# A two-block fp32 network on one core: products of zeros placed in TensorE's foreseen waits, and new tables for the order of the work

## The chip, the cores and the metric

One core of a Trainium2 chip runs the whole network as one program. The metric is device time in microseconds (us) of one execution; less is better. The kernel before has a median of 2796.93 us over three runs, the lowest 2793.36, the highest 2799.09.

## The reference

Batch 1, 512 tokens, width 1024, all in fp32. A first block: a mixer (dilated causal attention beside HGRN2, 8 heads each) and a mixture of experts. Then a second block with two layers over the same 512 tokens and 256 tokens of context: an even layer (MLA attention beside gated linear attention, GLA) and an odd layer (gated delta net, GDN), each with an MLP of width 4096.

```python
def first_block(x, ...):
    h = rmsnorm(x, norm1_g[layer])
    proj = h @ w_in[layer]
    ...
    mixed = jnp.concatenate([y_attn, y_hgrn], axis=-1)
    x = x + mixed @ w_out[layer]
    h2 = rmsnorm(x, norm2_g[layer])
    x = x + hier_moe(h2, ...)
    return rmsnorm(x, norm_f_g)

def second_block(x, c, ctx, ...):
    for layer in range(2):
        ml = jnp.split(silu(c) @ ada_w[layer] + ada_b[layer], 6)
        mc = jnp.split(silu(c_ctx) @ ada_w[layer] + ada_b[layer], 6)
        a_lat = modulate(rms_norm(h_lat, norm1_w[layer]), ml[0], ml[1])
        a_ctx = modulate(rms_norm(h_ctx, norm1_w[layer]), mc[0], mc[1])
        o_lat, o_ctx = even_mixer(...) if layer == 0 else odd_mixer(...)
        h_lat = h_lat + ml[2] * o_lat
        h_lat = h_lat + ml[5] * sq_relu_mlp(modulate(rms_norm(h_lat, norm2_w[layer]), ml[3], ml[4]), ...)
        ...
    return rms_norm(h_lat, final_norm)
```

`hier_moe` picks one group of 8 experts out of 4 for each token and in it the best two experts, and runs SwiGLU experts of width 512 on the tokens that chose them, in blocks of 128.

## The kernel before

Activations lie transposed in SBUF: features on the 128 partitions, tokens along the free dimension. Large products are made from three fp32r products each: activation and weight are split into a high part in fp32r and the rest (`xh`, `xl` and `wh`, `wl`), and xh·wh, xl·wh and xh·wl are summed in PSUM. A weight comes as a tile `raw` of 128x512 fp32 (256 KB) from memory; ScalarE (ACT) makes `wh` by a cast and VectorE (DVE) `wl` by a subtraction. The experts' weights (`mw`) and those of the modulation (`aw`) are used as they are, in fp32. All transfers but the gathers go out on SyncE's queue (SP); the gathers of token rows (`xg`) are indirect transfers that GpSimd (POOL) issues. A norm's sum of squares is a product of the squares `sq` with a matrix of ones (`const_all`), a pair of products to a norm of 128x512.

No engine's order is written by hand. Class `Rec` stands in for the engines: each operation is recorded as a `Unit` with its engine, its cost, its operands' tiles and a rank of the part it belongs to (table `RK`). `Rec.schedule` is a list scheduler: it runs a model of the five engines, takes at each step the unit that can start first on an engine (by rank, by order, by the weights in `ORDER`), honours limits on how many tiles of a name a part may hold (table `CAPS`), and returns one order of all units. It foresees when each unit starts, with a model of TensorE's clock among it. `Rec.flush` then emits the units in this order, so that each engine runs its instructions in it; every recorded operation is issued from one line, L336 in `emit` (L346 in the changed kernel). What an engine finds not ready it waits for, with everything behind it.

There are two flushes. The first part holds the mixer (`mix1`), the experts (`moe`, with the parts `ada0`, `evenC` and six of eight parts of the context's first MLP, `mlpC`, recorded among them as other work) and ends in a loop over overflow blocks (L1347) that runs zero times here. The second part holds `comb` (the sum of the experts' outputs), `evenL`, `ada1`, `mlpD` (the other two parts of mlpC), `oddC`, `mlp0`, `oddL` (GDN over the 512 tokens), `mlp1` and `end` (the final norm).

PSUM has 8 banks, all of one tag; each tile `pq` is a target of products. In the order's rows below, names carry the number of their tile.

Of the kernel before, what the change touches and what calls it, by code (L numbers as in the profile page):

```python
# [7 lines left out]
F32 = mybir.dt.float32  # L8
F32R = mybir.dt.float32r
# [7 lines left out]
P = 128  # L17
# [225 lines left out]
class Eng:
# [7 lines left out]
class Rec:  # L251
# [30 lines left out]
    def call(self, eng, method, a, k):  # L282
# [11 lines left out]
        out = writes[0] if writes else reads[0]  # L294
# [32 lines left out]
        u.uses += [(r, False) for r in reads] + [(w, True) for w in writes]
# [142 lines left out]
    def schedule(self):  # L470
# [33 lines left out]
        mode = None  # L504
# [28 lines left out]
        while len(order) < N:  # L533
# [112 lines left out]
    def flush(self):  # L646
# [233 lines left out]
class B:  # L880
# [9 lines left out]
    def start(self):  # L890
# [1371 lines left out]
def prep2(inp):  # L2262
# [20 lines left out]
    for z in range(2):  # L2283
# [29 lines left out]

RK = {"ada0": (7.4, 12.23), "ada1": (2.99, 8.19), "comb": (0.87, -1.0), "end": 3.3, "evenC": (1.97, 5.86),
      "evenC.gla": (-0.22, 6.0), "evenC.mla": (0.78, 7.24), "evenC.out": (6.2, 7.24), "evenL": (1.45, -0.02),
      "evenL.gla": (2.99, 2.44), "evenL.mla": (6.32, 0.83), "evenL.out": (4.6, 5.81), "mix1": (1.08, -0.1),
      "mix1.attn": (1.38, 5.7), "mix1.hgrn": (1.28, 7.3), "mix1.out": (6.5, 4.8), "mix1.qkv": (1.28, 2.69), "mlp0":
      (2.43, 5.08), "mlp1": (1.09, 6.3), "mlpC": (0.68, -0.4), "mlpD": (-0.31, -1.2), "moe": (1.04, 12.78), "oddC":  # L2320
      (6.88, 2.34), "oddC.inv": (0.63, 8.01), "oddC.inv0": (2.85, 6.33), "oddC.inv1": (5, 6.3), "oddC.opd": (4.6,
      8.42), "oddC.step": (4.6, 4.43), "oddC.v": (7.67, 8.09), "oddL": (1.79, 0.87), "oddL.g": (3.37, 2.62),
      "oddL.inv": (2.71, 3.97), "oddL.inv0": (1.66, -1.69), "oddL.inv1": (-1.23, -1.0), "oddL.opd": (12.48, 6.4),
      "oddL.out": (1.79, 0.8), "oddL.q": (5.6, 2.12), "oddL.step": (1.97, -0.27), "oddL.v": (-1.1, 0.9), "zero":
      (-0.31, 9.99)}
CAPS = {".xc": 68, ":x2561": 15, "ada0.ar": 153, "ada0.pq": 3, "ada0:pq": 13, "ada1.aw": 18, "ada1.pq": 11, "ada1:t":
      11, "comb.pq": 21, "comb.rs": 34, "comb.ru": 99, "comb.sq": 12, "comb.yy": 17, "comb:pq": 3, "comb:t": 204,
      "end.pq": 34, "end.rs": 11, "end.ru": 9, "end.sq": 4, "end.y": 36, "end:pq": 508, "end:t": 4, "evenC.ao": 66,
      "evenC.cqk": 68, "evenC.gA": 10, "evenC.gS": 8, "evenC.gb": 1, "evenC.gg": 24, "evenC.gkN": 10, "evenC.gke": 11,
      "evenC.gki": 1, "evenC.go": 5, "evenC.gqk": 6, "evenC.gt": 14, "evenC.gv": 4, "evenC.kT": 7, "evenC.kpe": 11,  # L2330
      "evenC.kx": 45, "evenC.ms": 24, "evenC.pT": 24, "evenC.pb": 90, "evenC.pq": 189, "evenC.qT": 2, "evenC.raw": 3,
      "evenC.rs": 33, "evenC.ru": 1, "evenC.s": 4, "evenC.sg": 25, "evenC.sq": 22, "evenC.vN": 9, "evenC.wh": 2,
      "evenC.wl": 51, "evenC.xh": 22, "evenC.xl": 72, "evenC:pq": 4, "evenC:s": 3, "evenC:t": 26, "evenL.gA": 17,
      "evenL.gS": 7, "evenL.gb": 15, "evenL.gg": 10, "evenL.gkN": 10, "evenL.gke": 1, "evenL.go": 17, "evenL.gst": 47,
      "evenL.gt": 49, "evenL.gv": 8, "evenL.kT": 541, "evenL.kc": 176, "evenL.kpe": 13, "evenL.kx": 26, "evenL.ms": 2,
      "evenL.pT": 8, "evenL.pa": 125, "evenL.pb": 12, "evenL.pq": 20, "evenL.qT": 4, "evenL.qps": 6, "evenL.raw": 3,
      "evenL.s": 11, "evenL.sg": 25, "evenL.sq": 56, "evenL.vc": 13, "evenL.wh": 2, "evenL.wl": 72, "evenL.y": 8,
# [7 lines left out]
      2, "mlp1:pq": 67, "mlpC.hl": 19, "mlpC.pq": 7, "mlpC.raw": 4, "mlpC.rl": 12, "mlpC.rs": 12, "mlpC.ru": 5,  # L2345
      "mlpC.sq": 11, "mlpC.wh": 6, "mlpC.xh": 42, "mlpC.xl": 28, "mlpC.y": 36, "mlpC:pq": 37, "mlpC:t": 58, "mlpD.hh":
      5, "mlpD.hl": 6, "mlpD.pq": 34, "mlpD.raw": 2, "mlpD.rl": 1265, "mlpD.wh": 41, "mlpD.wl": 63, "mlpD.xh": 23,
      "mlpD.xl": 4, "mlpD:pq": 1, "moe.BV": 12, "moe.EV": 128, "moe.RO": 3, "moe.RV": 48, "moe.hidT": 3, "moe.hr": 17,
      "moe.lT": 1, "moe.pq": 21, "moe.rs": 13, "moe.rt": 17, "moe.ru": 12, "moe.sg": 69, "moe.sq": 9, "moe.xg": 44,
      "moe.ys": 18, "moe:m4x": 11, "moe:m4y": 8, "moe:pq": 25, "oddC.A": 23, "oddC.Ax": 17, "oddC.G": 79, "oddC.TTx":  # L2350
      369, "oddC.Tx": 8, "oddC.Z": 7, "oddC.chb": 17, "oddC.hA": 3, "oddC.hB": 16, "oddC.hT": 137, "oddC.hp": 12,
      "oddC.kN": 9, "oddC.kP": 22, "oddC.kT": 3, "oddC.kbg": 1, "oddC.ke": 24, "oddC.kx": 12, "oddC.lab": 15,
      "oddC.pq": 28, "oddC.raw": 5, "oddC.rq": 52, "oddC.rs": 108, "oddC.ru": 5, "oddC.s": 32, "oddC.sg": 145,
      "oddC.u": 66, "oddC.vP": 12, "oddC.vT": 18, "oddC.vb": 19, "oddC.vs": 17, "oddC.wh": 25, "oddC.wl": 6,
      "oddC.wx": 58, "oddC.xl": 41, "oddC.y": 19, "oddC:pq": 7, "oddC:s": 14, "oddC:t": 45, "oddC:z4": 13, "oddL.A":
      7, "oddL.Ax": 38, "oddL.D": 7, "oddL.G": 15, "oddL.S": 76, "oddL.Tx": 18, "oddL.Z": 29, "oddL.eg": 56,
      "oddL.gT": 5, "oddL.gm": 40, "oddL.gn": 71, "oddL.hA": 10, "oddL.hT": 11, "oddL.hs": 22, "oddL.kN": 22,
      "oddL.kP": 120, "oddL.kT": 16, "oddL.kbg": 48, "oddL.ke": 17, "oddL.kx": 125, "oddL.o": 48, "oddL.pq": 74,
      "oddL.qP": 11, "oddL.qT": 78, "oddL.qkx": 9, "oddL.qx": 5, "oddL.raw": 7, "oddL.ri": 3, "oddL.rq": 1, "oddL.rs":
      65, "oddL.ru": 6, "oddL.s": 94, "oddL.sg": 13, "oddL.sq": 11, "oddL.u": 14, "oddL.vP": 15, "oddL.vT": 11,  # L2360
      "oddL.vb": 36, "oddL.vs": 14, "oddL.wh": 40, "oddL.wl": 57, "oddL.wx": 5, "oddL.xh": 70, "oddL.xl": 67,
      "oddL:pq": 8, "oddL:s": 6, "oddL:z4": 19, "zero.zero": 6, "zero:t": 34}
# [95 lines left out]
```

## Time and profile before

| | |
|---|---|
| median of 3 runs | 2796.93 us (2793.36 to 2799.09) |
| profiled execution | 2799.62 us |
| span of its instructions | 2797.8 us |
| mean granted clock of TensorE | 0.958 |
| busy: PE, DVE, ACT, POOL | 93%, 55%, 39%, 19% |
| moved by DMA | 503.39 MB, mean 180 GB/s |

The profiled execution is one run with its own time; the span runs from its first instruction to its last. PE is TensorE, PEld its loading of the stationary operand. A clock of 1.00 is 2.4 GHz, 0.50 is 1.2 GHz; a value between them for a stretch is a mean of the two. In a timeline, the end of a product is modelled; how fast products follow each other is read from their starts.

### The profile page before, as it was taken

The numbers are of one execution on the slowest core, as the hardware profiler recorded it, in microseconds if no ns is written. First come the engines' busy times: TensorE is split into PE (matmuls) and PEld (weight loads), VectorE is DVE, ScalarE is ACT, GpSimd is POOL, SyncE is SP. The second block draws the span as 40 slices with busy tenths as digits, with TensorE's granted clock in tenths as the row PEclk, the third lists the DMA queues.
The fourth block names the chain that finished last, engine by engine and source line by source line (L and its number), as shares of the span: only waits on it lengthen the run. The fifth ranks groups of instructions, "written<-read, shape, count | busy, mean of one in ns | idle before, by whom it ended". The sixth has DMA issues, their size and how long they took to land. (4 is left out here: it accounts for less than half of the span.)

```text
span 2797.8 us, 42711 instructions
## 1 busy us (share of the span) xinstructions
PE 2600.4 (93%) x15498; PEld 1906.0 (68%) x15498; DVE 1534.4 (55%) x2837; ACT 1096.3 (39%) x2243; POOL 518.2 (19%) x620
## 2 busy tenths in 40 slices
PE   7999989899999997999899998999898797899997
PEld 5875645445566664678657877888776686688886
DVE  7466432245343334846686875445668858454434
ACT  5346212235332323534455543333464525343321
POOL 1320013010010001112001321100143775010100
PEclk9999989999999999999799999999999788999999
DMA  5137799999999999931102545233324732233221
GB/s 196 54 110 241 271 308 321 298 307 326 379 340 365 378 367 328 380 126 55 47 22 75 171 118 163 85 106 102 93 96 106 193 95 73 79 106 106 87 83 42
DMA packets 323752, 503.39 MB, mean 180 GB/s; under 512 B 79826, under 2 KB 94162, under 8 KB 323026
## 3 DMA queue, kind: packets, MB, share of 16 engines
q1 hardware_dynamic: 318930, 492.23, 53.0%
q0 software_dynamic: 4608, 8.40, 0.8%
q8 instruction: 123, 2.02, 0.3%
q14 instruction: 91, 0.75, 0.1%
HBM read 473.22 MB, written 35.66 MB: 182 GB/s over the span
## 5 line engine op out<-in xcount | busy, mean ns | idle before, releaser
L336 PE MATMUL pq<-xh,wh 128*128 128x512 f32 (+1 forms) x1712 | 630.1, 368 | 33.2 <-ACT xh L336 14.3
L336 PE MATMUL pq<-xh,wl 128*128 128x512 f32 (+1 forms) x1712 | 615.8, 360 | 17.7 <-DVE wl L336 17.6
L336 ACT CAST wh<-raw 128x512 fp32r<-128x512 f32 x676 | 400.0, 615 | 560.4 <-DMA raw<-mlp_w 294.8
L336 PE MATMUL pq<-xl,wh 128*128 128x512 f32 (+1 forms) x1712 | 615.3, 359 | 3.6 <-DVE xl L336 3.6
L336 DVE TENSOR_TENSOR wl<-raw,wh 128x512 fp32r<-128x512 f32 (+1 forms) x676 | 478.4, 732 | 241.3 <-ACT wh L336 159.6
L336 PEld LDWEIGHTS pq<-xh,wh 128*128 128x128 f32 x1712 | 329.0, 192 | 120.3 <-ACT xh L336 33.6
L336 PEld LDWEIGHTS pq<-xh,wl 128*128 128x128 f32 x1712 | 328.5, 192 | 70.9 <-DVE wl L336 23.9
L336 PEld LDWEIGHTS pq<-xl,wh 128*128 128x128 f32 x1712 | 328.6, 192 | 52.4 <-DVE xl L336 5.7
L336 PE MATMUL pq<-hh,wh 128*128 128x512 f32 (+1 forms) x768 | 274.1, 357 | 0.0
L336 PE MATMUL pq<-hl,wh 128*128 128x512 f32 (+1 forms) x768 | 271.4, 353 | 0.0
L336 PE MATMUL pq<-hh,wl 128*128 128x512 f32 (+1 forms) x768 | 271.4, 353 | 0.0
L336 PE MATMUL pq<-mw,xT 128*64 128x512 f32 x1024 | 257.2, 611 | 0.7 <-DMA mw<-w_up 0.7
L336 DVE SCALAR_TENSOR_TENSOR x<-pq,mod,x 128x512 f32<-128x512 f32 x144 | 108.0, 750 | 225.4 <-PE pq L336 225.3
L336 POOL TENSOR_TENSOR rl<-rl 128x512 f32<-128x512 f32 (+1 forms) x96 | 100.2, 1049 | 702.5 <-ACT rl L336 621.2
L336 PEld LDWEIGHTS pq<-hh,wh 128*128 128x128 f32 x768 | 144.8, 189 | 35.9 <-issue 9.2
L336 PEld LDWEIGHTS pq<-hl,wh 128*128 128x128 f32 x768 | 144.9, 189 | 20.1 <-issue 0.2
L336 PEld LDWEIGHTS pq<-hh,wl 128*128 128x128 f32 x768 | 144.9, 189 | 20.0
L336 PEld LDWEIGHTS pq<-mw,xT 128*64 128x64 f32 x1024 | 70.8, 139 | 126.1 <-issue 91.5
L336 PE MATMUL pq<-mw,hidT 128*64 128x512 f32 x512 | 135.9, 604 | 3.2 <-DMA mw<-w_down 2.7
L336 DVE TENSOR_TENSOR hl<-rl,hh 128x512 fp32r<-128x512 f32 (+1 forms) x96 | 68.4, 721 | 97.8 <-ACT hh L336 81.6
L336 ACT ACTIVATE rl<-pq 128x512 f32<-128x512 f32 (+1 forms) x96 | 49.1, 525 | 164.6 <-PE pq L336 164.5
L336 ACT ACTIVATE sq<-x 128x512 f32<-128x512 f32 x64 | 39.2, 629 | 165.2 <-DVE x L336 127.7
(387 smaller groups left out, 3690.0 us busy)
## 6 DMA issues: line engine op xcount, KB each, us to landing
raw<-mlp_w SPq DMA_DIRECT2D x384, 256.0 KB
mw<-w_gate SPq DMA_DIRECT2D x256, 256.0 KB
mw<-w_up SPq DMA_DIRECT2D x256, 256.0 KB
mw<-w_down SPq DMA_DIRECT2D x256, 256.0 KB
aw<-ada_w SPq DMA_DIRECT2D x192, 256.0 KB
raw<-even_w_in SPq DMA_DIRECT2D x72, 256.0 KB
raw<-gdn_w_in SPq DMA_DIRECT2D x72, 256.0 KB
raw<-w_in SPq DMA_DIRECT2D x56, 256.0 KB
```

Source lines behind the costliest of these rows:

```text
L336: return getattr(getattr(self.real, eng), method)(*[f(v) for v in a], **kw)
```

## The change

It does three things. `Rec.call` gives each unit of PE that starts a tile of at least 256 columns (on 128 or 64 partitions) a price for a product of zeros of its shape. `Rec.schedule`, where it foresees that PE will stand idle for over 500 ns ahead of such a unit, puts a number of such products there: as many as fill 0.65 of the foreseen wait, at twice the price if the modelled clock is low, and books them as activity in its model of the clock. `Rec.flush` emits them ahead of the unit, with the unit's own output tile as their target; the unit's first product starts that tile anew, so they leave nothing behind. The zeros are two constant tiles. And the tables `RK`, `CAPS` and one weight of each pair in `ORDER` are new.

```diff
+FILL, SHARE = 500.0, 0.65
...
+            u.fill = (0, 0.0, 0.0)
+            if eng == "tensor" and len(out.shape) == 2 and k.get("start", True) and out.shape[0] in (64, 128):
+
+                n, full = int(out.shape[1]), out.shape[0] == 128
+                if full and n >= 256:
+                    u.fill = n, 13.3 + n / 2.4, n / 2.4
+                elif n >= 256:
+                    u.fill = n, max(224.0, 5.0 + n * 1.667), n / (0.6 if full else 1.2)
+            u.fills = 0
...
             if e == "tensor":
+                if u.fill[0] and st - eng[e] > FILL:
+
+                    slow = 1.0 if all(x[3] for x in clock) else 2.0
+                    u.fills = int(SHARE * (st - eng[e]) / (u.fill[1] * slow))
+                    for i_ in range(u.fills):
+                        at = eng[e] + i_ * u.fill[1] * slow
+                        for g, x in enumerate(clock):
+                            while x[0] < int(at / WINDOW + 0.25 * g):
+                                x[:] = x[0] + 1, x[2], 0.0, x[1] > WARM * WINDOW
+                            x[1] += u.fill[2]
...
             for i in order:
-                for c in self.units[i].calls:
+                u = self.units[i]
+                for _ in range(u.fills):
+                    o = u.calls[0][2][0]
+                    w, x = self.zeros[o.shape[0] == 128 and o.shape[1] >= 256]
+                    self.emit("tensor", "matmul", (o, w[:, :o.shape[0]], x[:, :o.shape[1]]),
+                              dict(start=True, stop=True, skip_group_check=True))
+                for c in u.calls:
                     self.emit(*c)
...
+        z, zr = (self.cp.tile([P, 512], t, name=f"zero{i}") for i, t in enumerate((F32, F32R)))
+        nc.gpsimd.memset(z, 0.0)
+        nc.vector.tensor_copy(zr, z)
+        nc.zeros = [(z, z), (zr, zr)]
...
-RK = {"ada0": (7.4, 12.23), "ada1": (2.99, 8.19), "comb": (0.87, -1.0), "end": 3.3, "evenC": (1.97, 5.86),
+RK = {"ada0": (5.47, 2.26), "ada1": (5.51, 3.96), "comb": (5.41, -0.59), "end": (5.65, 4.62), "evenC": (1.9, 2.93),
...
-CAPS = {".xc": 68, ":x2561": 15, "ada0.ar": 153, "ada0.pq": 3, "ada0:pq": 13, "ada1.aw": 18, "ada1.pq": 11, "ada1:t":
+CAPS = {".xc": 47, ":x2560": 5, "ada0.ar": 1, "ada0.aw": 246, "ada0.pq": 29, "ada0:pq": 75, "ada0:t": 32, "ada1.ar":
...
-ORDER = (9900, 3.991), (3500, 0.097)
+ORDER = (9900, 2.382), (3500, 0.093)
```

Over the whole program PE gets 151 products of zeros at 17 places (106 of 128x512, 41 of 128x256, 4 of 64x512), DVE one copy and POOL one memset; nothing else is added or taken away. 41 of the zeros stand in the first part, 110 in the second. Three places show what moved.

The first gather, on PE, where the routing of the tokens (`rt`, `ar`, `EV`, `BV`) ends and the first gathered rows `xg` are transposed by a product with the unit matrix. Before:

```order
L336 MATMUL pq_3615<-rt_3598,const_all 128x32 x7
L336 MATMUL pq_3661<-const_all,ar_3413 128x128 x4
L336 MATMUL pq_3674<-const_all,ar_3436 128x128 x4
L336 MATMUL pq_3686<-EV_3610,RO_3679 64x16 x32
L336 MATMUL pq_3781<-BV_3763,RV_3758 64x32 x8
L336 MATMUL pq_3831<-const_all,xg_3567 128x128 x4
L336 MATMUL pq_3838<-const_all,xg_3567 128x128 x4
```

Nothing stands between the routing and the first `xg`. In the changed kernel:

```order
L346 MATMUL pq_3673<-rt_3657,const_all 128x32 x7
L346 MATMUL pq_3614<-xh_3455,wh_3563 128x256
L346 MATMUL pq_3614<-xl_3559,wh_3563 128x256
L346 MATMUL pq_3614<-xh_3455,wl_3699 128x256
...
L346 MATMUL pq_3742<-EV_3691,RO_3731 64x16 x32
L346 MATMUL pq_3837<-BV_3817,RV_3812 64x32 x8
L346 MATMUL pq_3614<-xh_3466,wh_3736 128x256
L346 MATMUL pq_3614<-xl_3567,wh_3736 128x256
L346 MATMUL pq_3614<-xh_3466,wl_3848 128x256
...
L346 MATMUL pq_3933<-const_all,xg_3628 128x128 x4
L346 MATMUL pq_3942<-const_all,xg_3628 128x128 x4
```

Products of evenC (`xh`, `xl` with `wh`, `wl`, 128x256) now stand between the routing and the first transposes: 6 ahead of `EV`, and 42 between `BV` and the first `xg` (three of the 42 are shown).

The mixer's output, on PE, from the sum of squares (`sq`) of its norm to the first product of the output matrix (`xh,wh`). Before:

```order
L336 MATMUL pq_2435<-aw_2473,adasc 32x512
L336 MATMUL pq_2435<-aw_2481,adasc 32x512
L336 MATMUL pq_2891<-sq_2562,const_all 128x512
L336 MATMUL pq_2299<-aw_2496,adasc 32x512
L336 MATMUL pq_2299<-aw_2515,adasc 32x512
...
L336 MATMUL pq_2435<-aw_2825,adasc 32x512
L336 MATMUL pq_2435<-aw_2837,adasc 32x512
L336 MATMUL pq_2986<-xh_2948,wh_2872 128x512
```

Twelve small products of the modulation (`aw`) stand between the two. In the changed kernel, from the same sum of squares on:

```order
L346 MATMUL pq_2682<-hA_631,iN_857 64x128
L346 MATMUL pq_2718<-sq_2167,const_all 128x512
L346 MATMUL pq_2682<-hT_659,S_2626 64x32 x2
L346 MATMUL pq_2682<-hT_659,S_2680 64x32 x6
L346 MATMUL pq_2682<-hA_553,iN_810 64x128
L346 MATMUL pq_2682<-hA_631,iN_810 64x128
L346 MATMUL pq_2736<-vm_1487,t_2686 64x256 x2
L346 MATMUL pq_2736<-vm_1541,t_2686 64x256 x2
L346 MATMUL pq_2747<-hT_692,t_2123 128x128 x4
```

In their place stand HGRN2's products (`hT`, `hA`, `vm`), and they go on behind the last row shown here.

The end of GDN, on PE: its last products (`qkx,u`), the sums of squares of its output's norm and the first products of its output matrix (`oh,wh`). Before:

```order
L336 MATMUL pq_22773<-qkx_22750,u_22689 128x128
L336 MATMUL pq_22826<-sq_22820,const_all 128x512
L336 MATMUL pq_22833<-sq_22824,const_all 128x512
L336 MATMUL pq_22927<-oh_22429,wh_22853 128x512
L336 MATMUL pq_22927<-oh_22444,wh_22853 128x512
```

The sums of squares follow the last GDN products, and the output matrix follows them. In the changed kernel, first the same place, then, behind the output matrix, the norm ahead of mlp1 and its first product:

```order
L346 MATMUL pq_22870<-qkx_22810,u_22783 128x128
L346 MATMUL pq_22927<-zero_87 128x512 x16
L346 MATMUL pq_22927<-sq_22922,const_all 128x512
L346 MATMUL pq_22948<-sq_22925,const_all 128x512
L346 MATMUL pq_23048<-zero_87 128x512 x11
L346 MATMUL pq_23048<-oh_22549,wh_22968 128x512
...
L346 MATMUL pq_23333<-zero_87 128x512 x6
L346 MATMUL pq_23333<-sq_23154,const_all 128x512
L346 MATMUL pq_23333<-sq_23330,const_all 128x512
L346 MATMUL pq_23381<-zero_87 128x512 x17
L346 MATMUL pq_23381<-xh_23365,wh_23361 128x512
```

Only the products of zeros are new here: 16 and 11 around the first sums of squares, 6 and 17 around the second.

## Rows read from the trace of the kernel before

**Rows 1.** The page: busy time, and PE's granted clock in 40 slices.

```profile
PE 2600.4 (93%) x15498; PEld 1906.0 (68%) x15498; DVE 1534.4 (55%) x2837; ACT 1096.3 (39%) x2243; POOL 518.2 (19%) x620
...
PEclk9999989999999999999799999999999788999999
```

**Rows 2.** The waits of PE over the span: total us, times, longest.

```profile
PE pq L336 <- DMA xg<-h2d,idx: 18.8, 4, 8.4
PE pq L336 <- DVE sq L336: 18.8, 4, 12.8
...
PE pq L336 <- DMA mw<-w_down: 2.7, 4, 1.5
```

**Rows 3.** Stretches: from:to, us, PE, PEld, DVE, ACT, POOL, clock, DMA share, GB/s.

```profile
350.00:630.00 280.00, 253.13 (x1434) 139.69 (x1434) 93.00 (x230) 71.24 (x151) 47.71 (x63) 0.91 0.91 309
700.00:1050.00 350.00, 346.34 (x2124) 219.28 (x2122) 134.14 (x244) 108.81 (x215) 25.79 (x33) 1.00 1.01 366
2356.00:2371.50 15.50, 4.84 (x8) 1.54 (x6) 12.54 (x29) 10.27 (x38) 6.86 (x15) 0.60 0.13 41
2434.00:2779.00 345.00, 345.00 (x1523) 285.64 (x1522) 159.25 (x229) 114.43 (x197) 42.06 (x34) 1.00 0.27 86
```

**Rows 4.** Timeline of PE, 2416 to 2430: start, us, instruction, [idle before, releaser].

```profile
2419.48 2.91 PE L336 MATMUL pq<-sq,const_all 128*128 128x512 f32 x4 [2.24 <-DVE sq L336]
2427.54 0.80 PE L336 MATMUL pq<-xh,wh 128*128 128x512 f32 x1 [5.16 <-ACT xh L336]
...
2429.31 0.63 PE L336 MATMUL pq<-xh,wl 128*128 128x512 f32 x1
2429.73 0.63 PE L336 MATMUL pq<-xh,wh 128*128 128x512 f32 x1
```

**Rows 5.** Timeline of PE behind the loop, 1079 to 1097.

```profile
1091.97 0.58 PE L336 MATMUL pq<-xh,wh 128*128 128x256 f32 x1 [12.63 <-DMA xv<-mlpx]
...
1094.31 0.41 PE L336 MATMUL pq<-xh,wh 128*128 128x256 f32 x1
1094.52 0.41 PE L336 MATMUL pq<-xl,wh 128*128 128x256 f32 x1
...
1096.39 0.28 PE L336 MATMUL pq<-xh,wl 128*128 128x256 f32 x1
1096.51 0.28 PE L336 MATMUL pq<-xh,wh 128*128 128x256 f32 x1
```

**Rows 6.** Timeline of PE at the start, 0 to 30.

```profile
12.84 3.78 PE L336 MATMUL pq<-sq,const_all 128*128 128x512 f32 x4 [12.84 <-DVE sq L336]
23.16 0.80 PE L336 MATMUL pq<-xh,wh 128*128 128x512 f32 x1 [6.54 <-ACT xh L336]
25.10 0.80 PE L336 MATMUL pq<-xl,wh 128*128 128x512 f32 x1 [1.15 <-DVE xl L336]
```

**Rows 7.** Timeline of PE, sums of squares in the GDN part, at 2155.

```profile
2155.34 1.88 PE L336 MATMUL pq<-sq,const_all 128*128 128x512 f32 x4
```

**Rows 8.** Timeline of PE at the mixer's output, 276 to 283.

```profile
280.95 0.49 PE L336 MATMUL pq<-xh,wh 128*128 128x512 f32 x1 [2.65 <-ACT xh L336]
282.88 0.49 PE L336 MATMUL pq<-xl,wh 128*128 128x512 f32 x1 [1.44 <-DVE xl L336]
```

**Rows 9.** Timeline of PE at the first gather.

```profile
378.85 0.87 PE L336 MATMUL pq<-const_all,xg 128*128 128x128 f32 x3 [8.41 <-DMA xg<-h2d,idx]
```

**Rows 10.** The page: products of the experts' up and gate weights.

```profile
L336 PE MATMUL pq<-mw,xT 128*64 128x512 f32 x1024 | 257.2, 611 | 0.7 <-DMA mw<-w_up 0.7
```

**Rows 11.** Timeline of PE at 1361.

```profile
1370.44 0.80 PE L336 MATMUL pq<-xh,wl 128*128 128x512 f32 x1 [9.02 <-DVE wl L336]
```

**Rows 12.** Timeline of PE at the end of GDN, 2356 to 2371.

```profile
2360.66 3.78 PE L336 MATMUL pq<-sq,const_all 128*128 128x512 f32 x4 [4.39 <-ACT sq L336]
2370.64 1.69 PE L336 MATMUL pq<-oh,wh 128*128 128x512 f32 x2 [6.20 <-ACT oh L336]
```

**Rows 13.** Timeline of PE at the final norm.

```profile
2781.70 3.31 PE L336 MATMUL pq<-sq,const_all 128*128 128x512 f32 x4 [2.24 <-DVE sq L336]
```

More of the change, by code (lines that the diff above doesn't have):

```diff
@@ L233 @@
 class Unit:
-    __slots__ = ("eng", "calls", "cost", "lat", "pred", "succ", "uses", "prio", "npred", "ready", "start", "key", "idx", "refs", "ph", "rank", "late", "part", "need", "extra", "rows", "end", "mode")
+    __slots__ = ("eng", "calls", "cost", "lat", "pred", "succ", "uses", "prio", "npred", "ready", "start", "key", "idx", "refs", "ph", "rank", "late", "part", "need", "extra", "rows", "end", "mode", "fill", "fills")
 LAT = 200.0
@@ L2311, in prep2 @@
     return r
-RK = {"ada0": (7.4, 12.23), "ada1": (2.99, 8.19), "comb": (0.87, -1.0), "end": 3.3, "evenC": (1.97, 5.86),
[L2317 to L2325, printed above, removed]
@@ L2326 @@
-CAPS = {".xc": 68, ":x2561": 15, "ada0.ar": 153, "ada0.pq": 3, "ada0:pq": 13, "ada1.aw": 18, "ada1.pq": 11, "ada1:t":
[L2327 to L2337, printed above, removed]
[7 rows of a table removed]
[L2345 to L2362, printed above, removed]
@@ L2363 @@
-ORDER = (9900, 3.991), (3500, 0.097)
+RK = {"ada0": (5.47, 2.26), "ada1": (5.51, 3.96), "comb": (5.41, -0.59), "end": (5.65, 4.62), "evenC": (1.9, 2.93),
+      "evenC.gla": (1.9, 6.7), "evenC.mla": (0.15, -0.71), "evenC.out": (0.86, 1.74), "evenL": (3.9, 1.53),
+      "evenL.gla": (5.27, 3.96), "evenL.mla": (5.69, 5.62), "evenL.out": (5.51, 0.75), "mix1": (0.02, -0.83),
+      "mix1.attn": (2.48, -0.83), "mix1.hgrn": (3.14, 7.25), "mix1.out": (1.8, -0.73), "mix1.qkv": (0.93, 1.1),
+      "mlp0": (3.89, 4.72), "mlp1": (1.81, 3.77), "mlpC": (0.11, 5.2), "mlpD": (2.3, -0.8), "moe": (0.4, 6.71),
+      "oddC": (6.01, -0.9), "oddC.inv": (2.52, 5.62), "oddC.inv0": (4.2, 5.52), "oddC.inv1": (5, 6.3), "oddC.opd":
+      (4.6, 7.48), "oddC.step": (4.6, 1.08), "oddC.v": (6.01, 6.43), "oddL": (3.66, -1.25), "oddL.g": (3.84, 3.78),
+      "oddL.inv": (4.2, 5.52), "oddL.inv0": (2.78, -0.83), "oddL.inv1": (2.66, 0.06), "oddL.opd": (7.21, 3.87),
+      "oddL.out": (1.33, 6.12), "oddL.q": (5.16, 2.88), "oddL.step": (7.09, 6.8), "oddL.v": (1.73, 0.17), "zero":
+      (1.91, 7.47)}
@@ new lines @@
+CAPS = {".xc": 47, ":x2560": 5, "ada0.ar": 1, "ada0.aw": 246, "ada0.pq": 29, "ada0:pq": 75, "ada0:t": 32, "ada1.ar":
+      49, "ada1.aw": 11, "ada1.pq": 65, "ada1:pq": 21, "ada1:t": 8, "comb.pq": 45, "comb.rs": 11, "comb.ru": 12,
+      "comb.sq": 71, "comb.yy": 22, "comb:pq": 4, "comb:t": 10, "end.pq": 2, "end.rs": 25, "end.ru": 15, "end.sq": 6,
+      "end:pq": 1, "end:t": 4, "evenC.ao": 9, "evenC.cqk": 10, "evenC.gA": 10, "evenC.gS": 12, "evenC.gg": 6,
+      "evenC.gkN": 40, "evenC.gke": 40, "evenC.gki": 6, "evenC.gqk": 2, "evenC.gst": 1, "evenC.gt": 21, "evenC.gv":
+      52, "evenC.kT": 27, "evenC.kpe": 5, "evenC.kx": 18, "evenC.ms": 1, "evenC.pT": 245, "evenC.pb": 127, "evenC.pq":
+      5, "evenC.qT": 7, "evenC.raw": 3, "evenC.rs": 2, "evenC.ru": 1, "evenC.s": 20, "evenC.sg": 22, "evenC.sq": 6,
+      "evenC.wh": 2, "evenC.wl": 18, "evenC.xh": 88, "evenC.xl": 5, "evenC:pq": 47, "evenC:s": 20, "evenC:t": 26,
+      "evenL.ao": 28, "evenL.gS": 91, "evenL.gg": 61, "evenL.gkN": 52, "evenL.gke": 5, "evenL.gki": 7, "evenL.go": 54,
+      "evenL.gqk": 58, "evenL.gst": 2, "evenL.gt": 9, "evenL.gv": 21, "evenL.kT": 36, "evenL.kc": 10, "evenL.kpe": 6,
+      "evenL.kps": 45, "evenL.kx": 101, "evenL.ms": 2, "evenL.pT": 15, "evenL.pa": 46, "evenL.pb": 3, "evenL.pq": 63,
+      "evenL.qT": 4, "evenL.qps": 1, "evenL.raw": 3, "evenL.rs": 15, "evenL.s": 14, "evenL.sg": 35, "evenL.sq": 14,
+      "evenL.vN": 9, "evenL.vc": 27, "evenL.wh": 2, "evenL.wl": 36, "evenL.xh": 63, "evenL.xl": 89, "evenL.y": 8,
[8 rows of a table added]
+      6, "mlpC.rl": 6, "mlpC.rs": 5, "mlpC.wh": 2, "mlpC.wl": 16, "mlpC.xl": 40, "mlpC.xv": 6, "mlpC.y": 1, "mlpC:pq":
+      8, "mlpD.hh": 27, "mlpD.pq": 20, "mlpD.raw": 2, "mlpD.rl": 11, "mlpD.wh": 45, "mlpD.wl": 28, "mlpD.xh": 6,
+      "mlpD.xl": 7, "mlpD.xv": 8, "mlpD:t": 21, "moe.BV": 7, "moe.EV": 2, "moe.RV": 66, "moe.h": 30, "moe.hidT": 9,
+      "moe.hr": 2, "moe.lT": 20, "moe.pq": 17, "moe.rs": 34, "moe.ru": 126, "moe.sg": 3, "moe.sq": 14, "moe.xg": 80,
+      "moe.ys": 38, "moe:m4x": 20, "moe:m4y": 68, "moe:pq": 27, "oddC.A": 6, "oddC.G": 26, "oddC.S": 18, "oddC.TTx":
+      7, "oddC.Z": 7, "oddC.ab": 19, "oddC.chb": 1, "oddC.hA": 6, "oddC.hB": 9, "oddC.hT": 53, "oddC.hp": 14,
+      "oddC.kN": 52, "oddC.kP": 13, "oddC.kbg": 1, "oddC.ke": 426, "oddC.kx": 10, "oddC.lab": 3, "oddC.pq": 24,
+      "oddC.raw": 5, "oddC.rs": 4, "oddC.ru": 7, "oddC.s": 53, "oddC.sg": 4, "oddC.sq": 8, "oddC.u": 7, "oddC.vP": 50,
+      "oddC.vT": 12, "oddC.vb": 19, "oddC.vs": 4, "oddC.wh": 12, "oddC.wl": 6, "oddC.wx": 23, "oddC.xh": 8, "oddC.y":
+      5, "oddC:pq": 7, "oddC:s": 43, "oddC:t": 56, "oddC:z4": 4, "oddL.A": 7, "oddL.Ax": 18, "oddL.G": 8, "oddL.S": 8,
+      "oddL.TTx": 39, "oddL.Tx": 6, "oddL.Z": 90, "oddL.ab": 4, "oddL.gT": 2, "oddL.gg": 15, "oddL.gm": 15, "oddL.gn":
+      79, "oddL.hA": 132, "oddL.hB": 10, "oddL.hT": 13, "oddL.hp": 22, "oddL.hs": 34, "oddL.kP": 22, "oddL.kT": 11,
+      "oddL.kbg": 2, "oddL.ke": 56, "oddL.kx": 1, "oddL.o": 15, "oddL.pq": 22, "oddL.qP": 18, "oddL.qT": 26,
+      "oddL.qkx": 36, "oddL.qx": 36, "oddL.raw": 7, "oddL.ri": 4, "oddL.rq": 1, "oddL.rs": 75, "oddL.ru": 35,
+      "oddL.s": 83, "oddL.sg": 12, "oddL.sq": 18, "oddL.u": 3, "oddL.vP": 10, "oddL.vT": 154, "oddL.vb": 54,
+      "oddL.vs": 10, "oddL.wh": 18, "oddL.wl": 36, "oddL.wx": 8, "oddL.xh": 8, "oddL.xl": 25, "oddL.y": 51, "oddL:pq":
+      10, "oddL:z4": 31, "zero.zero": 27}
```

15 rows, old and new, of the table CAPS are left out of this document.

## The prediction

> **What bounds the kernel now.** Read the page's busy shares first: TensorE (PE) is busy for 93% of the span, no other engine reaches 60%, and the clock row says that it ran at full rate in nearly every slice [rows 1]. So the time is PE's work plus what PE loses, and it loses in two ways: it stands still, or it runs at half clock after standing still. The waits of PE by what they waited for come next [rows 2]: no single one is large. The two that head the list are 18.8 us, over four places each, and the one for a weight tile of the experts is 2.7. Third, the stretches [rows 3]. From 2434 to 2779 PE is busy all the time at clock 1.00, in 1523 products of 345.00 us, so 0.227 us each. Just ahead of it, 2356 to 2371.5 has 4.84 us of work in 15.5 us at clock 0.60. A microsecond saved ahead of the long stretch reaches the end whole, because nothing behind it waits for anything but PE. Between 700 and 1050 it is not so plain: PE is busy 346 of 350 us, but the DMA engines are too (share 1.01, 366 GB/s).
>
> The timeline gives the price of a cold clock [rows 4]: after a 5.16 us wait the products of 128x512 begin 0.42 us apart (2429.31, 2429.73), against 0.227 warm, so each cold one costs 0.20 more. For 128x256 it is 0.21 cold and 0.12 warm [rows 5].
>
> **The change part by part.** It adds 151 products of zeros at 17 places (106 of 128x512, 41 of 128x256, 4 of 64x512), a memset, a copy, and another order: the first part's is largely new, the second part's nearly the old one. The sum is made against the profiled execution, 2799.62 us, which is 2.7 above the median of the runs.
>
> *Start.* PE waits 12.84 us for the first squares, runs the first sums of squares in 3.78 us, and waits 6.54 and 1.15 us for the first operands [rows 6]. The 17 zeros ahead take 7.3 us at the cold price and the 10 behind 4.3 us, so both fit inside the waits. What they can give back: a pair of sums of squares that takes 1.88 us at a warm place [rows 7] could save 1.9, and some 14 cold products 0.20 each, 2.8; together 4.7. DVE must first make the zeros; if that pushes its own chain, it costs up to 2. I take **-3** (-4.7 to +2): the first fill ends before its wait does, so the clock may fall again.
>
> *Mixer's output.* Before, 12 small products stand between the sum of squares and the first output product, and PE waits 2.65 and 1.44 us there [rows 8]; then it runs some 8 products cold, 1.6 us. In the new order a long run of hgrn products stands between the two. The waits and the cold go, 5.7 at most; the hgrn products were cover elsewhere, so **-4** (-5.7 to 0).
>
> *First gather.* After the routing, PE waits 8.41 us for the gathered rows [rows 9]. The new order puts 48 products of evenC (6 + 42, at 0.12 us: 5.8 us) between the routing's products and the first transposes. The wait should shrink to some 3, and the clock recovers sooner: **-6** (-10 to 0). The three later gathers, 10.4 of the 18.8 us [rows 2], keep short covers and stay as they are.
>
> *Zeros among the experts.* 4 of 64x512 and 10 of 128x256. The expert products are fp32 and leave 1024 records, two a product, in 257.2 us [rows 10], so 0.50 us each: 4 x 0.50 + 10 x 0.12 = 3.2 if no wait is there, 0 if it is. I take **+2**. The 14 zeros ahead of mlpD cost 1.7 likewise; **+1**.
>
> *Loads of the experts.* Counting the weight tiles that PE uses along its order, the 280 us of PE work from 320 on use 474 tiles in the new order and 414 in the old: 60 tiles of 256 KB more, 15.7 MB. The stretch 350 to 630 moved 309 GB/s, and 366 was reached later [rows 3]; the difference over 280 us is 16.0 MB. So the loads just fit, if they run at the later rate while the gathers go on. The later stretch has 60 fewer, but PE time lost early isn't given back there, since PE was full. I take **+6** (0 to +24). The Trainium skill, "DMA: Bandwidth & Descriptors", Specifications, gives some 358 GB/s as a core's share of HBM, less than the measured 366; by it 13.7 MB would fit and 2.0 MB be late, an estimate of 5.6 us, about the same term.
>
> *Loop and second part.* At 1079 PE waits 12.63 us for a transfer, and the next 20 products run cold [rows 5]. The 17 zeros end within 4 us, long before the wait; **-0.5** (-1.8 to 0). At 1361 it waits 9.02 us for a wl [rows 11]; 23 zeros take 5.2, so the clock may last or not: 13 cold products, 2.6 us; **-1.5** (-2.6 to 0). In the GDN part a few products are put ahead of those that waited for transfers (TTx, Ax); **-3** (-8 to +5), the widest bound for the least that I can follow in it.
>
> *The end of GDN and the start of the last MLP.* Here are four waits in a row: 4.39 and 6.20 [rows 12], 2.24 and 5.16 [rows 4]. The sums of squares behind the first and third take 3.78 and 2.91 us, against 1.88 warm [rows 7]: 1.9 + 1.0. Behind the second and fourth some 13 and 14 products run cold: 2.6 + 2.8. Together 8.3. The zeros (16, 11, 6, 17) take 3.6, 2.5, 1.4 and 3.9 us warm, each less than its wait. Each wait itself stays, since it is a chain on ACT and DVE. All of it reaches the end: **-7** (-8.3 to 0). The final norm: 3.31 against 1.88 [rows 13], with 6 zeros ahead: **-1**.
>
> Sum: -3 - 4 - 6 + 2 + 1 + 6 - 0.5 - 1.5 - 3 - 7 - 1 = -17, so 2782.6 for that execution and **2780** against the median.
>
> What hides what: the zeros are free only as long as the wait they sit in is as long as foreseen. PE takes its instructions in order, so a zero ahead of an operand that is already there delays it by 0.12 to 0.50 us. The zeros write the tile that the next product starts anew, so they also need that PSUM tile free earlier, which at the places named it is: PE waits for an operand there, not for a bank.
>
> **The rivals.**
> *A, as above: 2780.*
> *B, the zeros don't hold the clock.* They stand at the front of a wait and fill 0.65 of its foreseen length, so PE is idle again when the operand comes; or zeros don't count. Then the start, 1361, the end of GDN and the final norm give nothing (12.5 us), and little is lost otherwise: 2792. For it: at 1361 and at the loop some 4 and 9 us stay empty behind the zeros, and no run here shows a product of zeros. Against it: at the end of GDN only 0.8 to 3.7 us stay empty, and after the 2.65 us wait at the mixer's output the first product took 0.49 us, against 0.80 after the 5.16 us wait [rows 4, 8]. The Trainium skill, "TensorE: Matmul & The Clock Gate", Part 1, says that activity releases the throttle, and that a limiter of another kind, driven by current, isn't tripped by zeros; by it zeros count as activity and case A stands, which no trace here shows yet.
> *C, the early experts become bound by loads, and the kernel slower.* If the loads stay at the 309 GB/s of that stretch, 15.7 MB take 51 us more, of which the 27 us in which PE did not work there (253.13 of 280 busy [rows 3]) are to be had: +24 instead of +6, and the gather's 6 us are eaten too, since a late tile is waited for anyway: 2780 + 18 + 6 = 2804. It decides once the rate over 350 to 630 stays below some 350 GB/s. For it: DMA share 0.91 already at 309, so the engines had little time left. Against it: the loads start ahead into many buffers, and PE waited hardly anywhere for a weight tile [rows 2].
> *D, the new first part is better than I can follow*, its other waits and cold runs go too: 20 us more, 2760.
>
> **How the numbers follow.** A change of 0.2% (5.6 us) is about what a measurement tells from none. A has 0.45 (its own range 2768 to 2792), B 0.22, C 0.22, D 0.11. A lies below 2791.3 nearly always, B half the time (else within 0.2%), C slower in four cases of five (else within). That is 0.64 faster, 0.18 the same, 0.18 slower. The range for 8 in 10 runs from 2752, short of most of D's tail, to 2808, C with a little more lost.
>
> **What would show it.** Right: clock near 1.00 in the stretch 2350 to 2430 (shifted) and its sums of squares near 1.9 us; the first wait for xg at some 3 us; no wait at the mixer's output; waits for a mw tile of a few us in all; DMA near 360 GB/s through the early experts. B: products behind the zeros 0.42 us apart. C: many short waits of PE for mw or for a wh and wl, PE busy well below 95% between 350 and 650. Wrong altogether, if a wait of 10 us or more appears where neither order shows a reason, as in GDN.

## The result: slower by 0.54%

The changed kernel takes 2809.35 us (median of 8 runs), the kernel before 2796.30 us beside it (8 runs): a ratio of 1.0054, 95% interval 1.0035 to 1.0074. Ratios here and below are the recorded ones, with their 95% intervals in brackets; the quotient of the two medians is not the same number (here 1.0047) and differs from them by up to 0.0018, so a difference of 0.001 between two ratios says nothing. The forecast was 2780, faster by 0.6%, with a range of 2752 to 2808. The profiled execution of the change is one of 2810.28 us, near its median. The two lines of its page that answer to [rows 1]:

```profile
PE 2642.3 (94%) x15653; PEld 1942.7 (69%) x15653; DVE 1531.8 (55%) x2838; ACT 1095.3 (39%) x2243; POOL 508.0 (18%) x621
...
PEclk9999989999999998999899999999999799999999
```

PE is busy 41.9 us longer than before, most of it with the zeros, and the span is 10.7 us longer: the work that was added, zeros above all, fills more than the waits gave back. The waits of PE, as in [rows 2]:

```profile
PE pq L346 <- DMA xg<-h2d,idx: 13.7, 5, 6.6
PE pq L346 <- DVE wl L346: 13.5, 9, 3.4
...
PE pq L346 <- DVE sq L346: 5.9, 4, 3.9
PE pq L346 <- ACT xh L346: 5.6, 4, 3.6
...
PE pq L346 <- DVE hA L346: 3.4, 2, 2.0
...
PE pq L346 <- DMA mw<-w_down: 2.2, 1, 2.2
```

The waits for xg fell from 18.8 to 13.7 us and those for sq from 18.8 to 5.9, yet the kernel is slower: shorter waits are not a shorter path. The timeline of PE at the places that the prediction named, from the start to the end of GDN:

```profile
1.86 6.89 PE L346 MATMUL pq<-zero 128*128 128x512 f32 x17 [1.86 <-DVE zero L346]
12.64 3.78 PE L346 MATMUL pq<-sq,const_all 128*128 128x512 f32 x4 [3.90 <-DVE sq L346]
...
23.09 0.50 PE L346 MATMUL pq<-xh,wh 128*128 128x512 f32 x1 [3.58 <-ACT xh L346]
...
25.62 0.63 PE L346 MATMUL pq<-xh,wl 128*128 128x512 f32 x1
26.05 0.63 PE L346 MATMUL pq<-xh,wh 128*128 128x512 f32 x1
...
387.73 1.06 PE L346 MATMUL pq<-const_all,xg 128*128 128x128 f32 x8 [1.77 <-DMA xg<-h2d,idx]
...
1094.63 4.00 PE L346 MATMUL pq<-zero 128*128 128x256 f32 x17 [6.00 <-ACT s L346]
1098.94 0.58 PE L346 MATMUL pq<-xh,wh 128*128 128x256 f32 x1 [0.32 <-ACT xh L346]
...
2368.17 3.92 PE L346 MATMUL pq<-zero 128*128 128x512 f32 x16
2374.66 1.98 PE L346 MATMUL pq<-sq,const_all 128*128 128x512 f32 x4 [2.57 <-ACT sq L346]
2376.08 3.08 PE L346 MATMUL pq<-zero 128*128 128x512 f32 x11
2383.70 1.70 PE L346 MATMUL pq<-oh,wh 128*128 128x512 f32 x2 [4.54 <-ACT oh L346]
...
2386.47 0.63 PE L346 MATMUL pq<-oh,wl 128*128 128x512 f32 x1
2386.90 1.06 PE L346 MATMUL pq<-oh,wh 128*128 128x512 f32 x2
```

At the start the zeros run, and the first operand still comes at 23.09 (23.16 before [rows 6]), with products 0.43 us apart behind it. The first gathered rows are transposed at 387.73 after a wait of 1.77 us; before it was 378.85 after 8.41 [rows 9]: the wait is shorter and its end is later. Behind the loop the first product starts at 1098.94, against 1091.97 [rows 5]. At the end of GDN the sums of squares run at full rate (1.98 us), but 4.54 us stay empty behind the zeros, and the output matrix starts cold.

### The profile page after: what moved, and what is told of

Read it like the earlier page. It is cut to its first block, busy times and chain, and to the rows that moved or that the text cites. A ratio compares the mean times of both kernels' runs of the same rounds, so it can differ in the third digit from the quotient of the medians.

```text
span 2808.5 us, 43018 instructions
## 1 busy us (share of the span) xinstructions
PE 2642.3 (94%) x15653; PEld 1942.7 (69%) x15653; DVE 1531.8 (55%) x2838; ACT 1095.3 (39%) x2243; POOL 508.0 (18%) x621
## 5 line engine op out<-in xcount | busy, mean ns | idle before, releaser
L346 POOL TENSOR_TENSOR rl<-rl 128x512 f32<-128x512 f32 (+1 forms) x96 | 92.5, 972 | 719.2 <-ACT rl L346 674.5
```

Of the source, the lines that this page charges most:

```text
L346: return getattr(getattr(self.real, eng), method)(*[f(v) for v in a], **kw)
```

## The experiments

The first theory was T: the new order costs, the zeros give a little. Its rival Z: the zeros cost and the order doesn't. Four kernels take the tables of the two parts and the zeros apart (the lines that stand for the tables are shortened here).

**No zeros, new order (e1).**

```diff
-                for _ in range(u.fills):
+                for _ in range(0):
```

> The changed kernel's tables and order, word for word, with none of the 151 products of zeros emitted. Theory T (the new order costs, the zeros give a little): the first part stays about 8 us longer than before, the waits ahead of the first products of the output matrix and of mlp1 are cold again, so the time is 2812 us or a little more, ratio to before 1.005 to 1.009. Rival Z (the zeros cost, the order is neutral or better): the time falls to before's or below it, ratio 0.996 to 1.001.

Measured: 2805.84 us against 2790.56 (12 and 29 runs), ratio 1.0047 [1.0023, 1.0071]; close below theory T's 1.005 to 1.009, and not Z's.

**Zeros, old order (e2).**

```diff
-RK, CAPS, ORDER = (tables of the change)
+RK, CAPS, ORDER = (tables of before)
```

> The code of the change with the tables of before: the old order with 151 products of zeros at much the same places. Theory T: the zeros alone gain what they gain in the traces at the start (1.4 us), behind the loop (2.4), at 1361 (some 5) and from the end of GDN on (3.5), less some 3 for zeros among the experts: about 2787 us, ratio 0.995 to 0.999. Rival Z: 2805 us, ratio 1.002 to 1.005.

Measured: 2789.08 us, ratio 0.9998 [0.9979, 1.0017], between the two forecasts; 151 zeros again.

**Old first part, new second part, zeros (e3).**

```diff
-ranks and limits of mix1, moe, ada0, evenC, mlpC, and ORDER[0]: of the change
+ranks and limits of mix1, moe, ada0, evenC, mlpC, and ORDER[0]: of before
```

> The change with the first part's tables of before, the second part's new ones. If the whole loss lies in the first part's new order (8 to 9 us), the time is 2790, ratio 0.997. If the second part's new order costs too (the traces show a lag that grows by some 7 us between 1640 and 2220), the gain of the zeros and that loss cancel: 2797, ratio 1.000. Rival Z: 2805.

Measured: 2782.74 us, ratio 0.9972 [0.9950, 0.9994].

**New first part, old second part, zeros (e4).** The same edit for the phases of the second part.

> The change with the second part's tables of before, the first part's new ones. If the first part's order is what costs, ratio 1.001 to 1.004 (2799 to 2806): some 8 us lost in the first part, some 8 gained by zeros in the second. If the second part's order costs all of it, ratio 0.996.

Measured: 2810.64 us (6 runs), ratio 1.0072 [1.0046, 1.0098]; more than the 1.001 to 1.004 that was expected.

With both second parts, the new first part costs some 20 us: 1.0072 against 0.9998, and 1.0054 against 0.9972. In both pairs the intervals lie clear of each other. The new second part gains 5 to 7 by the ratios (0.9972 against 0.9998, 1.0054 against 1.0072), which lies within their uncertainty. The zeros do nothing that can be measured: 0.9998 in the old order, and in the new one 1.0054 with and 1.0047 without. Theory T holds in its first half and not in its second.

**Why the first part? Half loads (e5, e6).** Theory L was the prediction's rival C, late loads; theory P a loss on PE itself. Half of every expert weight is loaded, in both orders. The products read the left half of a tile twice, so the result is not the reference's, and the scheduler prices the half load as a whole one, so that the order stays:

```diff
+            if out.base.name.startswith("mw"):
+                c *= 2
...
-        nc.sync.dma_start(w, ap)
-        return w
+        nc.sync.dma_start(w[:, :256], ap[:, :256])
+        return w[:, None, :256].to_broadcast([P, 2, 256])
```

> The changed kernel in its own order, zeros too; each expert weight tile has only its left half loaded (128 KB instead of 256), and the products read that half twice, so the result isn't the reference's. Theory L (the new first part loses its 20 us to loads that come late): the loss goes, ratio to before 0.995 to 0.998, like the kernel with the old first part. Theory P (it loses them on PE itself: products that no longer run in pairs, cold stretches, waits on other engines): the loss stays, ratio 1.003 to 1.007.

> The same half loads with the first part in the old order (tables of before) and the second part in the new one. Theory L: little changes, since the old order had room: ratio 0.993 to 0.998, and the gap between the two orders shrinks from some 22 us to under 6. Theory P: ratio 0.995 to 0.998 and the gap between the orders stays at 15 us or more.

Measured: 0.9941 [0.9924, 0.9958] in the new order, 0.9904 [0.9888, 0.9920] in the old. The gap between the orders shrinks from 23 us to 10, which is neither theory's number. The timelines say more: from the routing's first product (362.5) to the last expert product (1088.0) the change takes 725.6 us, the kernel before 722.7, and with half loads it is 698.4 in the new order and 694.0 in the old. Halving the loads makes this stretch shorter by 27.2 and 28.7 us, so they cost both orders nearly the same. The stretch 350 to 630 of the changed kernel, as in [rows 3], has PE busy for 262.12 us (253.13 before) at 335 GB/s (309 before):

```profile
350.00:630.00 280.00, 262.12 (x1411) 138.38 (x1409) 81.34 (x198) 61.32 (x118) 40.73 (x49) 0.94 0.97 335
```

In the half-load profile of the new order the routing began at 375.3 instead of 362.5, at the same instruction. The stretch where that happened is the mixer, 222 to 262 us; the runs on it follow behind two others.

**No zeros, old first part, new second part (e8)**, the edit of e1 in e3, to have the zeros' worth in the other order too.

> Old tables in the first part, new ones in the second, and none of the zeros emitted. If the zeros give nothing (as the first pair of runs says), the time is that of the same kernel with zeros, 2783 us, ratio 0.996 to 0.999. If they give what I forecast from the places (12 us), ratio 1.000 to 1.002.

Measured: 0.9982 [0.9961, 1.0003]; the zeros are worth 0.1% here, inside the uncertainty.

**The mixer's tables alone as before (e7)**, ranks and limits of mix1.

> The changed kernel with the mixer's tables alone (ranks and limits of mix1) as before; the planner then finds a third order for the first part. If the loss is made in the mixer (pairs of 64-row products broken up there, 4.4 us by the trace, and what else comes with it), ratio 0.997 to 1.001. If it is made among the experts, ratio 1.004 to 1.008.

Measured: 1.0260 [1.0240, 1.0280]. The planner's third order starts the routing only at 427.5 us; it answers nothing about the other two.

**Pairs (e9).** In the new order products of the attention with 64-row operands no longer stand beside their partner. Groups of PE's instructions by shape (count, busy us, mean ns), before and after:

```profile
L336 PE MATMUL pq<-qk,qk 64*128 64x512 f32 x16 | 6.8, 628 | 0.0
```

```profile
L346 PE MATMUL pq<-qk,qk 64*128 64x512 f32 x16 | 9.9, 703 | 0.2 <-ACT pT L346 0.2
```

The edit sorts the finished order once more and puts such a product right behind its partner, where the two stand at most 25 places apart on PE:

```diff
+            d = row[s] - row[f]
+            if 1 < d <= NEAR:
+                key[f] = pos[s] - 0.5
```

> The new order without zeros (as e1_no_zeros, ratio 1.0047), but each product of 64-row operands of the attention (tiles qk) is put right behind its partner of the same shape, as the old order has them. By the traces of before and of the change those products take 12.1 us in pairs and 16.5 us apart. If the lost pairs are the first part's loss, the 4 us come back in the trace and the ratio falls to 1.003 or 1.0035; if the loss is elsewhere, the products take 12 us again and the time stays within 0.1% of 1.0047.

Measured: 1.0051 [1.0028, 1.0073]. The same products take 7.4 us, but the time does not follow: other waits of PE grew (21.9 us of idle from the first sum of squares to the routing, 15.8 in e1, the order without pairs and zeros). So pairs alone do not bring the loss back. What they are worth by themselves stays open, because the re-sorted order brought some 6 us of new waits with it.

**The clock in the mixer (e11, e13, e14).** In the new order PE waits 1.40 us at 220 us for hA, and the clock falls. Windows 222 to 262 of four executions (us, busy PE, PEld, DVE, ACT, POOL, clock, DMA share, GB/s): the change in the profile above, the same kernel in a second profile (e14_look_a) and in a third (e14_look_c), and a kernel with 8 zeros at this wait (e11):

```profile
222.00:262.00 40.00, 39.76 (x330) 22.94 (x332) 28.75 (x102) 26.03 (x65) 5.10 (x4) 0.91 0.55 179
```

```profile
222.00:262.00 40.00, 39.10 (x194) 18.73 (x196) 19.22 (x77) 15.34 (x44) 1.27 (x1) 0.57 0.23 76
```

```profile
222.00:262.00 40.00, 39.56 (x328) 22.69 (x328) 28.72 (x102) 25.93 (x65) 5.10 (x4) 0.91 0.54 174
```

```profile
222.00:262.00 40.00, 38.53 (x336) 23.02 (x336) 29.07 (x103) 26.15 (x65) 5.11 (x4) 1.00 0.52 180
```

Same program, same instructions: in one execution the granted clock is back at 2.4 GHz after 7 us, in another it stays at 1.2 GHz for 34, with PE busy for 39.10 of 40 us and only 194 products done instead of 330. What runs there (e14_look_a's timeline):

```profile
222.67 0.91 PE L346 MATMUL pq<-qk,qk 64*128 64x384 f32 x2 [1.41 <-DVE hA L346]
223.51 0.66 PE L346 MATMUL pq<-const_all,pr 128*128 128x128 f32 x4
...
229.36 0.69 PE L346 MATMUL pq<-const_all,pr 128*128 128x128 f32 x2
229.97 2.07 PE L346 MATMUL pq<-qk,qk 64*128 64x512 f32 x2
```

A fall at this place is not the new order's alone. With the old first part PE waits as long there, as in this line of e10:

```profile
225.81 0.33 PE L346 MATMUL pq<-const_all,pr 128*128 128x128 f32 x1 [1.45 <-DVE pr L346]
```

Behind that wait the clock is low for 3.4 to 13.7 us in five of six profiles of that order, and not at all in the sixth (the kernel before). What only the new order shows is the fall of 34 us.

The edit of e11: no zeros but 8 of 128x384 ahead of the product that waits there.

```diff
+        for u in self.units:
+            u.fills = {'pq482': 8}.get(u.key.name, 0) if u.eng == "tensor" and u.fill[0] else 0
```

> The new order without its zeros (as e1_no_zeros, ratio 1.0047) but with 8 zeros of 128x384 in the one wait of 1.40 us in the mixer, at 220 us, behind which the clock fell for 6.8 us in three profiles of this order and for 34 us in the fourth (half loads). If that fall is what makes the new order slow and uneven, it goes: no cold stretch at 220 to 260, ratio 1.001 to 1.003, a narrower spread than 2787 to 2818. If not, the ratio stays at 1.004 to 1.005 with the same spread.

Measured: 2793.48 us, ratio 1.0014 [0.9993, 1.0035], 2787 to 2807; no cold stretch there in its profile. The trace puts the same 1.40 us wait for hA ahead of these zeros, so they stand behind the wait, not in it; they take 1.6 us, and the time is still some 9 us lower than without them. To see whether that was chance, the same 8 zeros went into the change itself:

> The changed kernel, zeros and all (ratio 1.0054), with 8 more zeros of 128x384 ahead of the one attention product at 220 us. If the fall of the clock there is what makes the change slow, the ratio falls by what the same 8 zeros took off the order without zeros (1.0047 to 1.0014): 1.001 to 1.003, and the profile has no cold stretch between 215 and 260 us. If that was chance, it stays at 1.004 to 1.007.

Measured: 2797.10 us against 2790.05, ratio 1.0019 [1.0000, 1.0039], again some 10 us below the change. Each of the two differences alone is near the edge of its intervals; that they agree, and the profiles below, speak for them. Three more profiles of the change as it is:

> The changed kernel as it is, one more profile: does the clock, which falls at 223 us in every execution of this order, stay down for 7 us (as in three of the profiles with whole loads) or for 34 (as in the one with half loads)? If the long stretch is what the mended kernels lack, at least one of three such profiles shows it, with some 12 us on the first part; if none does, it is not what makes the change slow.

> As e14_look_a, a second execution: the same question, the same two answers (a cold stretch of 7 or of 34 us at 223).

> As e14_look_a, a third execution: the same question, the same two answers (a cold stretch of 7 or of 34 us at 223).

Two of the three show 34 us at half clock (225 to 259 us); with the half-load kernel that is three of the seven profiles of this order that have no zeros at this wait. The two executions took 2805.26 and 2806.95 us, the third 2797.56. The first product behind the loop, in the three:

```profile
1111.34 0.38 PE L346 MATMUL pq<-xh,wh 128*128 128x256 f32 x1 [2.49 <-ACT xh L346]
```

```profile
1115.04 0.38 PE L346 MATMUL pq<-xh,wh 128*128 128x256 f32 x1 [2.79 <-ACT xh L346]
```

```profile
1104.71 0.58 PE L346 MATMUL pq<-xh,wh 128*128 128x256 f32 x1 [1.96 <-ACT xh L346]
```

It starts at 1096.0 to 1098.9 in the three earlier profiles of this order with whole loads, and at 1088.4 to 1092.0 with the old first part. In e11 and e13 it is 1096.4 and 1100.0, hardly earlier than in the executions with the short fall. So by these few profiles the 8 zeros save mainly the long fall: 1113.2 against 1099.6 on average, some 13.5 us in three of seven executions. That is an estimate of 6 us per execution, of the 9 to 10 that the ratios give.

**Longer zeros at the end (e10).** As e3, with the numbers of zeros set to fill the waits that the profile without zeros shows:

```diff
+            for i, n in zip([i for i in order if self.units[i].fills], [17, 4, 7, 3, 36, 26, 26, 9, 22, 9]):
+                self.units[i].fills = n
```

> As e3_old_first (old first part, new second part, zeros; ratio 0.9972), but in the second part's later places as many zeros as fill the whole wait that the trace shows without zeros: 36 at 1361 (9.2 us), 26, 26, 9 and 22 from the end of GDN to the start of the last MLP (6.5, 6.2, 2.2, 5.2 us), 9 at the end. If zeros hold the clock and those of the change only ended too early, the output matrix and the first products of the last MLP start at full rate: some 5 us less, ratio 0.995. If zeros don't hold the clock at all, nothing changes or it is slower by what runs over.

Measured: 2781.60 us against 2793.06, ratio 0.9965 [0.9946, 0.9983]. The 0.9972 of e3 lies inside this interval, so the time does not show the further gain that was expected (0.995). Its timeline at the end of GDN and the start of the last MLP:

```profile
2344.43 6.18 PE L346 MATMUL pq<-zero 128*128 128x512 f32 x26
2351.16 1.98 PE L346 MATMUL pq<-sq,const_all 128*128 128x512 f32 x4 [0.55 <-ACT sq L346]
2352.58 6.50 PE L346 MATMUL pq<-zero 128*128 128x512 f32 x26
2360.20 0.51 PE L346 MATMUL pq<-oh,wh 128*128 128x512 f32 x1 [1.12 <-ACT oh L346]
...
2415.39 0.50 PE L346 MATMUL pq<-xl,wh 128*128 128x512 f32 x1 [0.67 <-DVE xl L346]
...
2418.64 0.50 PE L346 MATMUL pq<-xl,wh 128*128 128x512 f32 x1 [0.91 <-DVE xl L346]
```

In this execution the zeros held the clock where they lasted nearly as long as the wait: from 2343 to 2360 it is 1.00, and the output matrix, from its first to its last product, takes 44.2 us instead of 46.7 in e3. One profile is not the last word here either. In e6, with the change's own 16 and 11 zeros, the clock was low from 2336.6 to 2340.0, while the 11 zeros ran, and was back when the output matrix began, which takes 44.2 us there too:

```profile
2337.28 4.38 PE L346 MATMUL pq<-zero 128*128 128x512 f32 x11
2344.54 0.50 PE L346 MATMUL pq<-oh,wh 128*128 128x512 f32 x1 [2.88 <-ACT oh L346]
```

The last MLP's first 60 products take 17.0 us at full clock, and 17.2 in the kernel before with 13 of them cold [rows 4]: at full clock PE runs into waits for xl (0.67, 0.91 us), because DVE makes the operands no faster.

## Why the prediction was wrong

Point by point, by its own steps:

- **The first part's order is the step that failed.** The prediction found two waits there that the new order shortens (the mixer's output, the first gather), took -10 for them and +6 for loads, and let the rest of a largely rewritten order count as nothing; rival D had that rest as a gain only. Measured, that order costs some 20 us, and the time came out just above the range. About half of it goes with the fall of the clock at 220 us: 8 products of zeros at that one place took 9 to 10 us off in two kernels, by ratios whose difference is near the edge of the intervals. The rest is some 8 us by the first product behind the loop (1096.4 and 1100.0 in e11 and e13, 1088.4 to 1092.0 with the old first part), spread over the mixer (broken pairs may be among it) and the experts. Which instruction holds how much of the rest was not settled, nor was why the clock stays low for 34 us in one execution and for 7 in another.
- **First gather, -6:** right in size as a wait. 8.41 fell to 1.77 us, and all waits for xg from 18.8 to 13.7. But its end is 8.88 us later: the routing began 6.4 us later (362.5 against 356.1), and the 48 products now stand ahead of it.
- **Mixer's output, -4:** the two waits went, as forecast, but one of 1.97 us for hA stands ahead of it now, and the clock is low from 280.8 to 287.7.
- **Loads, +6 (rival C):** not seen as late loads. From the routing to the last expert product it is 722.7 before and 725.6 after (on average 721.7 in five profiles with the old first part and 726.0 in eight with the new one), and PE's waits for mw are 3.4 and 3.1 us. The rate over 350 to 630 rose from 309 to 335 GB/s. That is below the 350 at which C was to decide, and yet PE is busy for more of the stretch than before. C gave the sign and a time of 2804, close to the result, but by a mechanism that the runs don't show; that is luck.
- **Start, -3:** it came to nothing. The zeros ended, 3.90 us of wait remained, and the first sums took 3.78 us again. The first operands wait for ACT and DVE as before.
- **Loop, -0.5:** too small to see. From the last expert product to the next one it is 10.9 us in this profile, 13.2 before and 12.2 without zeros (e1); in the other profiles with zeros here it runs from 11.2 to 13.5.
- **1361, -1.5:** the 23 zeros (5.61 us) kept the clock up in this profile, over the 2.38 us that were left of the wait, and PE then waited 1.59 and 0.82 us for the next wl. In e13 and the three later profiles of the change 4.0 us were left, and the clock fell for 3.4 us. Where the products run at full rate they wait for DVE's wl, so little of the cold had cost time.
- **The end of GDN and the last MLP, -7:** mis-sized. Between the change and the same order without zeros (e1) the steps there differ by 1.6 us together (first sums to the output matrix 9.04 against 9.99, output matrix 46.8 against 46.4, second sums to the first operand 7.20 against 7.95, 60 products 16.99 against 17.32). From the last GDN product to the 61st product of the last MLP it is 90.2 to 90.7 us in the four profiles of the new second part without zeros there, 86.8 to 90.3 in eight with the change's zeros, and 86.8 in e10. Two reasons, which e10 and the change's profile show: the zeros ended before their wait did, so the clock fell behind them, and part of what the cold clock cost was hidden by operands that come at their own pace anyway.
- **Final norm, -1:** right. The last sums take 1.98 us instead of 3.31.
- **GDN's reorder, -3:** not contradicted. The new second part gains 5 to 7 us by the ratios, which is within their uncertainty; where, was not tried.
- **Zeros among the experts, +2 and +1:** not measured apart. All zeros together are worth between -0.1% and +0.1% in three pairs of kernels, which is nearest to rival B's account of them (12.5 us of gains that don't come). Of B's two reasons the first is what the profile shows, that PE is idle again behind the zeros when the operand comes. The second, that zeros don't count, is not what e10 shows. And at some of the places the cold clock had cost little to begin with.

Beside the runs, the Trainium skill's sentence that activity releases the throttle ("TensorE: Matmul & The Clock Gate", Part 1) agrees with e10, where zeros kept the clock at 1.00. It does not fit e14_look_a, where PE was busy for 39.10 of 40 us with small products and the clock stayed low for 34; there the measurement decides.

## What to carry to other kernels

When an order is rewritten, the waits that it visibly shortens are a small sample of it: price the rest as unknown in both directions. Don't count a shorter wait as a gain until its end is earlier. Before paying for a warm clock, ask whether the products behind the wait are bound by PE at all; where their operands come at another engine's pace, cold products cost little. And where small products follow a short wait, compare several executions: one profile may show a short fall of the clock and the next one a long one, as here with 7 and 34 us.

## What the runs showed of the hardware that was not expected

- The clock can stay at 1.2 GHz for 27 to 34 us while PE is busy with hardly a pause, in some executions and not in others of the same program. It happened at two places: in the mixer (above; 34.00 of 34 us busy in e14_look_a), and in GLA's products (29.30 of 30 us busy in the kernel before), where the profile of before and that of the change were cold from 1325 to 1355 and from 1336 to 1363 us, e6 for 30.7 us and the other kernels, each in its profile, for no longer than 3.4 us at this place. From the first product behind the loop to the end it is 1704 to 1710 us in those three executions and 1689 to 1698 in all others, so this is worth some 10 us as well; it is in the profile of before and in that of the change, so it does not separate those two. The same 16 products of GLA there, in the kernel before and in e8:

```profile
1330.27 3.67 PE L336 MATMUL pq<-gt,gS 64*128 64x64 f32 x16
```

```profile
1326.70 2.00 PE L346 MATMUL pq<-gt,gS 64*128 64x64 f32 x16
```

- Much of the spread between runs of one kernel goes with this clock. In e1 the 12 runs range from 2786.65 us at a mean clock of 0.965 to 2817.90 at 0.949, and time and clock correlate by -0.97; in e3 by -0.96, in the kernel before (29 runs) by -0.88. It is weaker elsewhere: -0.61 in e13 and -0.23 in the change's own 8 runs. A comparison of single executions of these kernels can be off by 10 us and more.
- Half the expert loads make the stretch of the experts 27 to 30 us shorter in both orders, though PE's recorded waits for these tiles are under 4 us. In the old order 7 of the 30 are waits for the gathers, which land sooner beside fewer loads, and 14 are shorter busy times of the expert products themselves. Part of both may be the clock, which was low for 37.5 us of the stretch in e6 and for 54.6 in e3.
